# Attention's second key half rotated earlier and split later, an output-weight split moved behind the masking, and three matmuls and two splits reordered at the seam before attention

## The chip, the core and the metric

The kernel runs on one core of a Trainium2 chip. That core has a matrix engine (PE, TensorE) and four more engines that each work through their own instruction queue in order: DVE (VectorE), ACT (ScalarE), POOL (GpSimd) and SP (SyncE, which only issues transfers here). Engines wait for each other by semaphores. The metric is the device time of one execution in microseconds (us), as the median of several runs. A small letter-number such as L1318 is a line of the kernel as the profile counts it.

## The reference, cut to what matters

Two layers on 512 tokens of width 1024 in float32: a gated short convolution with its feed-forward network (FFN0), then sliding-window attention with sinks, whose keys and values are computed once from the residual stream, with its own feed-forward network (FFN1).

```python
kv = rmsnorm(h, kv_norm) @ w_kv
k_sh, v_sh = jnp.split(kv, 2, axis=-1)
k_sh = partial_rotary(k_sh.reshape(bsz, s, N_KV_HEADS, HEAD_DIM), cos, sin)
q = (rmsnorm(h, b_pre_norm[j]) @ b_w_q[j]).reshape(bsz, s, N_HEADS, HEAD_DIM)
q = partial_rotary(q, cos, sin)
attn = sliding_window_sink_attention(q, k_sh, v_sh, b_sinks[j]) @ b_w_o[j]
h = h + rmsnorm(attn, b_post_norm[j])
```

There are 16 query heads of 64 columns on 4 key heads, blocks of 128 queries, and each query block sees its own and the previous block of keys. `sliding_window_sink_attention` adds the mask to the scaled scores, takes a softmax that has one more column for the sink, and weighs the values with it.

## The kernel before, in words

**Every product is three matmuls.** A float32 operand is split into a high part (rounded by a copy on ACT) and a low part (the rest, by a subtraction on DVE or POOL). A product is then low times high, high times high and high times low, which stand as three PE rows L192, L193, L194. "Splitting" below always means this pair: first the high part on ACT, then the low part elsewhere, which waits for it.

**The seam between FFN0 and attention.** `close` runs FFN0's last product tile by tile (four tiles t of 128 tokens, two halves each, four k-steps of three matmuls in the last half that is of interest). Behind it `last_tile` finishes the residual of tile 3: `norm(t)` writes the normalised rows `xn` on ACT (L326). PE transposes these (L337, into banks `xt`) in two lots: tiles 0 and 1 inside `close`, tiles 2 and 3 later, between the matmuls of the key and value projections (`pk`, `pv`). Each transposed bank is split twice, once with the gains of the keys and values (n = 0) and once with those of the queries (n = 1), by `split(n, f, half)`: the high part on ACT at L350, the low part on DVE at L351, for one eighth f of the width. Bank b of four holds the eighths f = b and f = b + 4.

**Attention's loop.** After the seam a loop runs over steps i = 0 to 9. Each step issues the operations of the string `ORDER` in its order, each for the head pair that its offset gives: `Q` project queries, `R` rotate them, `H` split the rotated ones, `S` scores, `M` mask and take the maximum, `E` exponents, `N` normalise, `T` transpose the probabilities, `P` and `L` their high and low parts, `W` weigh the values, `O` split the result. The number behind a letter is a half or a block. There is no planner behind it. The string is the order in which every engine gets its instructions, since the scheduling is set to manual there, and each engine's queue keeps that order.

- `rope` (rotation) is a shuffle of the projection (L1244) and a product with the cosines (L1246) on DVE, then a product with the sines (L1247) and a sum (L1248) on POOL. `rope_split` is a high part on ACT (L1253) and a low part on POOL (L1254).
- `K` rotates and splits the second half of the keys once, at i = 2. The head pairs 4 to 7 read it, from i = 4 on.
- `g0` and `g1` split part of the output weights early. At i = 4 these are whole tiles (L187 on ACT, L188 on DVE), at i = 6 they are halves in slots (L181, L182). `G` splits the query weights of a later pair with the same lines L187 and L188.
- The transient tiles (`sh`, `ra`, `rhi`, `rlo`, `plo` and others) come from one pool of 35 slots, which are handed out in turn. Whoever takes a slot waits until its last reader is done.

**Names the prediction uses.** M0 and M1 are the L1318 rows that read the score banks `psc` (each with a small row that reads out the maximum). S0 and S1 write those banks (L1306). N0 and N1 are L1346, L1348 and four L1351. T0 to T3 are the L1363 transposes into `pt`. L0 to L3 are the L1380 rows. W0 to W3 are the `po` matmuls.

Of the kernel before, what the change touches and what calls it, by code (L numbers as in the profile page):

```python
# [44 lines left out]

EARLY_IN, REST_IN = 2, 0
ORDER = (
    "R- S0 T0 g0 T1 O- Q0 M0 Q1 Z0 P0 P1 S1 T2 T3 L0 Q2 L1 G M1 E00 E01 H- Q3 P2 P3 E10 E11 Z1 z0 K W0 L2 L3 A A A N0 W1 W2 N1 W3 g1 z1"
)
STEP = {  # L50
    "S": "scores", "M": "maxima", "E": "exponents", "N": "normalise", "T": "turn", "P": "high",
# [22 lines left out]
def yoco_kernel(  # L74
# [22 lines left out]
    nc = tc.nc  # L97
# [458 lines left out]
    for l in range(2):  # L556
# [3 lines left out]
        for rd, (f0, f1) in enumerate(ROUNDS[:-1]):  # L560
            k = slice(f0 // 2, f1 // 2)
# [107 lines left out]
    with tc.manual_schedule(engines=ALL):  # L669
# [25 lines left out]
        for k in range(KT):  # L695
# [7 lines left out]
            for i in range(3):  # L703
                for t in range(3):
                    n = 3 * k + t
# [9 lines left out]
        ws = [split_weights(None, raw, True) for raw in later[:2]]  # L715
# [150 lines left out]
        if square:  # L866
            res.square(t)

    def close(ws, x, k0, res, ahead, then=None, each=2):


        n = len(x) - k0

        def part(ps, t, half, ks):
            unit(ps, t, ws[len(ws) // 2 * half :], x, ks, n, k0)

        begun = [bank("pmix", ps_mm) for _ in range(2)]
        for half in range(2):
            part(begun[half], 0, half, range(n - 1))
            for _ in range(each if half == 0 or each > 1 else 0):  # L880
                ahead.one()
        for t in range(NB):
            for half in range(2):
                if t == 0:
                    ps = begun[half]
                    part(ps, t, half, range(n - 1, n))
                else:
                    ps = bank("pmix", ps_mm)
                    if (t, half) == (NB - 1, 1):
                        part(ps, t, half, range(2))  # L890
                        for b in range(4):
                            res.turn(b, (0, 1))
                        part(ps, t, half, range(2, n))
                        for f in range(4):
                            res.split(0, f, 0)
                        res.square_mix(t, 0)
                        res.square(NB - 2)
                        res.scale(t, 0)
                    else:
                        part(ps, t, half, range(n))  # L900
                res.take(t, half, ps)
                if (t, half) != (NB - 1, 0):
                    res.square_mix(t, half)
            if t < NB - 1:
                tile_done(res, t, square=t < NB - 2)
            if t == 0 and then:
                then()

    def last_tile(res, pieces, ahead=None):


        def some(i):
            for n, *f in pieces[i]:
                if n == "keep":
                    res.keep(f[0], 0, f[1])
                elif n == "weights":
                    ahead.slots()
                else:
                    res.split(n, f[0], 0)

        res.mean2(2)
        res.norm(2)
        res.mean(3)
        res.scale(3, 1)
        some(0)
        res.update(3)
        some(1)
        res.square(3)
        some(2)
        res.mean2(3)  # L930
        some(3)
        res.norm(3)
        some(4)
# [30 lines left out]
    def ffn(l, before, ahead, gain, gpres, following):  # L964
# [220 lines left out]
        if gpres:  # L1185
            ahead = Ahead(following)
            with tc.manual_schedule(engines=ALL):
                close(ws, acts[-1], 0, res, ahead)
            return res, ahead
        with tc.manual_schedule(engines=ALL):  # L1190
            for t in range(NB):
# [59 lines left out]
    def rope_split(a, eng, large=False):  # L1251
        hi, lo = halves("rhl", F32R) if large else (slot("rhi", F32R), slot("rlo", F32R))
        nc.scalar.activation(hi, a, AF.Copy)  # L1253
        eng.tensor_tensor(out=lo, in0=a, in1=hi.bitcast(F32), op=ALU.subtract)  # L1254
        return hi, lo
# [170 lines left out]
    at = []  # L1426

    with tc.manual_schedule(engines=ALL):
        last_tile(res, [[(0, 4)], [(0, 5)], [], [(0, 6), (0, 7), (1, 0), (1, 1)],
                        [(1, f) for f in (4, 5, 2, 3, 6, 7)]])  # L1430
        for hf in range(2):
            c = slice(hf * 256, (hf + 1) * 256)
            for k in range(KT):
                kk = slice(k * P, (k + 1) * P)
                for ps, (whi, wlo) in zip(pk, wk):
                    mm3(ps[:, c], whi[:, kk], wlo[:, kk], xkv[k][0][:, c], xkv[k][1][:, c],
                        k == 0, k == KT - 1)
                values(2 * hf, k)
                values(2 * hf + 1, k)
                if hf == 0 and k >= 6:  # L1440
                    for b in (2 * k - 12, 2 * k - 11):
                        res.turn(b, (2, 3))
                        res.split(0, b, 1)
            if hf == 0:
                for f in range(4, KT):
                    res.split(0, f, 1)
            if hf == 0:
                ahead.one()
                for f in range(KT):
                    res.split(1, f, 1)  # L1450
                ahead.one()
                qs[0].w, qs[1].w = ahead.ready[4:]


        vt = [halves("vt", F32R) for _ in range(NB)]
        for pair in vt:
            for v in pair:
                nc.gpsimd.memset(v.bitcast(F32), 0.0)

        last_p = [slot("lp", F32R) for i in range(2)]  # L1460
        for p in last_p:
            nc.gpsimd.memset(p.bitcast(F32), 0.0)
        for part in range(4):
            qs[0].project(part)
        ks = [rope_split(rope(pk[0], nc.vector), nc.vector)]
        qs[LEAD].weights()
        nc.scalar.activation(warm, ones[:, 0:1], AF.Exp)
        for part in range(4):
            qs[1].project(part)
        qs[0].rotate(nc.vector)  # L1470
        qs[0].split(nc.vector)
        dst = [[v.rearrange("p (h d) -> p h d", d=2 * HD)[:, :, :HD] for v in pair]
               for pair in vt]
        src = [p.rearrange("p (h d) -> p h d", d=HD) for p in pv]
        for j in range(NB):
            nc.scalar.activation(dst[j][0], src[j], AF.Copy)
        for j in range(NB):
            nc.vector.tensor_tensor(out=dst[j][1], in0=src[j], in1=dst[j][0].bitcast(F32),
                                    op=ALU.subtract)

    with tc.manual_schedule(engines=ALL):
        sum_on("a0")
        for i in range(KT + 2):
            if i == KT:
                res = Update(mix_o, B_ATT, [G_FPRE[1]])
                res.leaves = True
                ahead = Ahead(first_weights(1))
            if i == KT + 1:
                res.load()
            for c in ORDER.split():  # L1490
                if c == "A":
                    if i == KT:
                        ahead.one()
                    continue
                if c == "K":
                    if i == 2:
                        ks.append(rope_split(rope(pk[1], nc.gpsimd), nc.gpsimd))
                    continue
                late = c.endswith("-")
                op, n = c[0], [int(d) for d in c[1:].rstrip("-")]  # L1500
                t = i - late
                if op == "g":

                    u = 2 * (t - EARLY - 1) + n[0]
                    if u in (-2, -1, 2, 3):
                        j = u + 2 if u < 0 else u
                        early_w.append(split_weights(w_o[j // 2, j % 2], slots=j >= EARLY_IN))
                    continue
                if op in "SMENTPLWO":
                    t -= op in "TPLWO"  # L1510
                    of = hp
                elif op in "QRH":
                    t += LEAD
                    of = qs
                elif op == "G":
                    t += LEAD + 1
                    of = qs
                    if KT <= t < KT + 4:
                        j = t - KT
                        rest_w.append(split_weights(w_o[j // 2, 2 + j % 2], slots=j >= REST_IN))  # L1520
                else:
                    t = 2 * (t - EARLY - 1) + n.pop(0)
                    of = early
                if 0 <= t < len(of) and not (op in "RH" and t < LEAD - 1):
                    getattr(of[t], STEP[op])(*n)
                if op in "RH" and i <= KT:
                    issue(len(issues) // 2 if op == "R" else len(issues))
            if i <= KT:
                sum_on(f"a{i + 1}")
        close(rest_w, at, EARLY, res, ahead, lambda: sum_on(f"a{KT + 2}"), 1)  # L1530
# [96 lines left out]
```

## Time and profile before

| what | value |
|---|---|
| median of 3 runs | 1023.06 us (1022.95 to 1023.82) |
| the profiled execution's own time | 1023.55 us |
| its span in the profile | 1021.8 us |
| granted TensorE clock, mean | 0.998 |
| busy: PE / DVE / ACT / POOL | 1011.7 / 869.4 / 582.3 / 197.3 us |

The profiled execution is 0.49 us longer than the median of the runs, and 1.75 us of its time lie outside the span. A row of a timeline gives the start in us from the span's start, the duration in us, engine, line, operation, what it writes and reads, its shape, how many alike follow each other ("x4"), and in brackets the idle time of its engine just before it with what ended that. PE rows overlap: matmuls are pipelined, so the distance between two starts is what a matmul costs, and a wait is a distance that is longer than it is for the same work elsewhere.

### The profile page before, as it was taken

Reading aid. Unit: us, or ns where it says so; the run is one execution under the profiler, and the core shown is the slowest. Engines: PE = TensorE matmul, PEld = TensorE weight load, DVE = VectorE, ACT = ScalarE, POOL = GpSimd, SP = SyncE. Lnnn points to the kernel's source line nnn. Section 1 sums busy time; section 2 is a strip of 40 time slices with the busy share of each in tenths; the row PEclk is TensorE's granted clock in tenths of the full one; section 3 lists DMA queues with packets and bytes.
Section 4 is the critical chain, followed back from the end, with each engine's and each line's share of the span. In section 5 each row is a group of like instructions: output and inputs, shape, how many; then the busy total and the mean of one; then the engine's idle time right before and its main releaser. Section 6 shows DMA issues by size and latency. Waiting matters only on the chain.

```text
span 1021.8 us, 16273 instructions
## 1 busy us (share of the span) xinstructions
PE 1011.7 (99%) x6008; PEld 893.5 (87%) x6008; DVE 869.4 (85%) x1480; ACT 582.3 (57%) x1035; POOL 197.3 (19%) x259
## 2 busy tenths in 40 slices
PE   9999999999999999999999999999999999999997
PEld 8888888999889898998898788889998998989986
DVE  5766767899789999998869998778997899999896
ACT  6322444875655455566476676668666564645641
POOL 0443033112111111000123663231111010110001
PEclk9999999999999999999999999999999999999999
DMA  9897789549979699779404889976899676979742
GB/s 357 284 263 227 179 253 341 161 165 283 344 242 298 208 300 339 221 217 337 167 6 160 187 220 299 249 249 160 261 296 328 176 238 226 296 271 268 257 155 83
DMA packets 66575, 244.50 MB, mean 239 GB/s; under 512 B 7872, under 2 KB 8384, under 8 KB 54720
## 3 DMA queue, kind: packets, MB, share of 16 engines
q1 hardware_dynamic: 51328, 145.98, 38.7%
q0 software_dynamic: 14592, 96.48, 37.2%
q10 hardware_dynamic: 576, 1.02, 0.3%
q8 instruction: 47, 0.77, 0.3%
q14 instruction: 32, 0.26, 0.1%
HBM read 237.15 MB, written 102.76 MB: 333 GB/s over the span
## 4 chain that ended last, share of the span: by engine, by line
PE 90%; DVE 5%; ACT 2%; issue 1%; POOL 0%; DVEq 0%; ACTq 0%
PE gx L1055 14%; PE gx L1058 7%; PE pcub L193 4%; PE pcub L194 4%; PE pcub L192 4%; PE gz L194 4%; PE gz L192 4%; PE gz L193 4%; PE px L192 3%; PE px L193 3%; PE px L194 3%; PE pmix L193 2%; PE pmix L192 2%; PE pmix L194 2%; PE gy L193 2%; PE gy L192 2%
## 5 line engine op out<-in xcount | busy, mean ns | idle before, releaser
L478 DVE TENSOR_TENSOR wlo<-raw,whi 128x1024 fp32r<-128x1024 f32 x225 | 274.7, 1225 | 54.5 <-ACT whi L477 54.4
L477 ACT ACTIVATE whi<-raw 128x1024 fp32r<-128x1024 f32 x225 | 233.7, 1051 | 103.5 <-DVE raw L465 29.2
L1055 PE MATMUL gx<-xt,whi 128*128 128x512 f32 x480 | 120.4, 393 | 0.0
L1055 PEld LDWEIGHTS gx<-xt,whi 128*128 128x128 f32 x480 | 86.3, 189 | 15.5
L546 POOL DMA_DIRECT2D hsum<-in_w_gb_dram x96 | 62.9, 735 | 150.2 <-ACT whi L477 89.9
L546 POOL DMA_DIRECT2D hsum<-hsum x32 | 25.4, 792 | 291.0 <-ACT whi L477 219.4
L1017 DVE TENSOR_TENSOR st<-gx,st 128x256 f32<-128x256 f32 x200 | 77.9, 419 | 2.6 <-ACT st L1033 0.5
L1033 ACT ACTIVATE st<-gx 128x256 f32<-128x256 f32 x120 | 43.2, 380 | 62.3 <-PE gx L1058 58.7
L1058 PEld LDWEIGHTS gx<-xt,wlo 128*128 128x128 f32 x480 | 65.5, 190 | 4.7
L1058 PE MATMUL gx<-xt,wlo 128*128 128x256 f32 x480 | 66.9, 282 | 0.0
L1069 ACT ACTIVATE gr<-gr 128x1024 f32<-128x1024 f32 x20 | 21.2, 1062 | 50.2 <-DVE gr L1017 50.2
L192 PE MATMUL px<-wlo,ahi 128*128 128x512 f32 x120 | 46.8, 390 | 0.1
L194 PE MATMUL px<-whi,alo 128*128 128x512 f32 x120 | 46.7, 389 | 0.0
L193 PE MATMUL px<-whi,ahi 128*128 128x512 f32 x120 | 46.7, 389 | 0.0
L194 PE MATMUL gz<-xhi,wlo 128*128 128x256 f32 x160 | 45.5, 284 | 0.0
L192 PE MATMUL gy<-xlo,whi 128*128 128x256 f32 x160 | 45.3, 283 | 0.0
L193 PE MATMUL gy<-xhi,whi 128*128 128x256 f32 x160 | 45.3, 283 | 0.0
L192 PE MATMUL gz<-xt,whi 128*128 128x256 f32 x160 | 45.3, 283 | 0.0
L193 PE MATMUL gz<-xt,whi 128*128 128x256 f32 x160 | 45.3, 283 | 0.0
L194 PE MATMUL gy<-xhi,wlo 128*128 128x256 f32 x160 | 45.3, 283 | 0.0
L192 PE MATMUL gz<-xlo,whi 128*128 128x256 f32 x160 | 45.3, 283 | 0.0
L194 PE MATMUL gz<-xt,wlo 128*128 128x256 f32 x160 | 45.3, 283 | 0.0
(298 smaller groups left out, 2999.4 us busy)
## 6 DMA issues: line engine op xcount, KB each, us to landing
hsum<-in_w_gb_dram POOLq DMA_DIRECT2D x96, 512.0 KB, 7.8
raw<-hsum SPq DMA_DIRECT2D x88, 512.0 KB, 7.8
raw<-in_w_gb_dram SPq DMA_DIRECT2D x60, 512.0 KB, 6.7
hsum<-in_w_dn_dram POOLq DMA_DIRECT2D x36, 512.0 KB, 8.1
raw<-in_w_dn_dram SPq DMA_DIRECT2D x32, 512.0 KB, 6.5
hsum<-hsum POOLq DMA_DIRECT2D x28, 512.0 KB, 5.4
raw<-in_w_in_dram SPq DMA_DIRECT2D x21, 512.0 KB, 7.6
hsum<-in_w_dn_dram POOLq DMA_DIRECT2D x12, 768.0 KB, 12.5
```

Source lines behind the costliest of these rows:

```text
L192: nc.tensor.matmul(out, whi, xlo, start=start, stop=False, **kw)
L193: nc.tensor.matmul(out, whi, xhi, start=False, stop=False, **kw)
L194: nc.tensor.matmul(out, wlo, xhi, start=False, stop=stop, **kw)
L477: self.begun = nc.scalar.activation(hi[:, :n], raw, AF.Copy)
L478: nc.vector.tensor_tensor(out=lo[:, :n], in0=raw, in1=hi[:, :n].bitcast(F32), op=ALU.subtract)
L546: nc.gpsimd.dma_start(dst, src, max_dma_last_dim=4 * 4 * S, **kw))
L1017: nc.vector.tensor_tensor(out=out, in0=a, in1=b, op=ALU.add)
L1033: nc.scalar.activation(ste, a, AF.Copy)
L1055: nc.tensor.matmul(banks[c][e], whi[:, kk], factors[p][k][2], start=opened and k == 0, stop=False, **kw)
L1058: nc.tensor.matmul(banks[c][e][:, :256], wlo[:, kk], factors[p][k][0], start=False, stop=k == 3 and p == 4, **kw)
L1069: nc.scalar.activation(kept[2], kept[2], AF.Silu)
```

## The change

```diff
 ORDER = (
-    "R- S0 T0 g0 T1 O- Q0 M0 Q1 Z0 P0 P1 S1 T2 T3 L0 Q2 L1 G M1 E00 E01 H- Q3 P2 P3 E10 E11 Z1 z0 K W0 L2 L3 A A A N0 W1 W2 N1 W3 g1 z1"
+    "R- S0 T0 T1 O- Q0 M0 Q1 Z0 P0 P1 S1 T2 T3 L0 Q2 L1 G K M1 E00 E01 H- k g0 Q3 P2 P3 E10 E11 Z1 z0 W0 L2 L3 A A A N0 W1 W2 N1 W3 g1 z1"
 )
...
-    def close(ws, x, k0, res, ahead, then=None, each=2):
+    def close(ws, x, k0, res, ahead, then=None, each=2, lead=2):
...
                     if (t, half) == (NB - 1, 1):
-                        part(ps, t, half, range(2))
+                        part(ps, t, half, range(lead))
                         for b in range(4):
                             res.turn(b, (0, 1))
-                        part(ps, t, half, range(2, n))
+                        part(ps, t, half, range(lead, n))
...
-                close(ws, acts[-1], 0, res, ahead)
+                close(ws, acts[-1], 0, res, ahead, lead=3)
...
-        last_tile(res, [[(0, 4)], [(0, 5)], [], [(0, 6), (0, 7), (1, 0), (1, 1)],
-                        [(1, f) for f in (4, 5, 2, 3, 6, 7)]])
+        last_tile(res, [[(0, 4)], [(0, 5)], [],
+                        [(0, 6), (0, 7), (1, 0), (1, 1), (1, 4), (1, 5)],
+                        [(1, f) for f in (2, 3, 6, 7)]])
...
                 if c == "K":
                     if i == 2:
-                        ks.append(rope_split(rope(pk[1], nc.gpsimd), nc.gpsimd))
+                        rot_k = rope(pk[1], nc.gpsimd)
+                    continue
+                if c == "k":
+                    if i == 3:
+                        ks.append(rope_split(rot_k, nc.gpsimd))
                     continue
```

Nothing is computed differently, and no instruction is added or removed. There are four moves. `K` now only rotates, ahead of `M1` at i = 2, and the new `k` splits, behind `H-` at i = 3. `g0` moves from ahead of `O-` and `M0` to behind `k`, which matters at i = 4 and at i = 6. At the seam the sixteen transposes of tiles 0 and 1 stand behind three instead of two of the four k-steps. And the query splits of eighths 4 and 5 stand ahead of `norm(3)` instead of behind it.

PE's queue at the seam, before (`pmix` is FFN0's last product, `xt_5168` and its successors are the transposed banks):

```order
L192 MATMUL pmix_5161<-wlo_4850,ahi_4613 128x512
L193 MATMUL pmix_5161<-whi_4848,ahi_4613 128x512
L194 MATMUL pmix_5161<-whi_4848,alo_4614 128x512
L337 MATMUL xt_5168<-ident,xn_5103 128x128
L337 MATMUL xt_5168<-ident,xn_5143 128x128
```

The same place in the changed kernel:

```order
L194 MATMUL pmix_5161<-whi_4848,alo_4614 128x512
L192 MATMUL pmix_5161<-wlo_4897,ahi_4839 128x512
L193 MATMUL pmix_5161<-whi_4895,ahi_4839 128x512
L194 MATMUL pmix_5161<-whi_4895,alo_4840 128x512
L337 MATMUL xt_5171<-ident,xn_5103 128x128
L337 MATMUL xt_5171<-ident,xn_5143 128x128
```

One k-step of three matmuls now lies ahead of the first transpose. `xn_5103` and `xn_5143` are the normalised tiles 0 and 1.

ACT's queue a little later at the seam, as a piece of the difference (`xn_5257` before and `xn_5265` after is the normalised tile 3, `xt_5168` or `xt_5171` is bank 0, `xt_5173` or `xt_5176` bank 1):

```order
-L326 ACTIVATE xn_5257<-h_5000,ur_4990 128x1024
-L350 ACTIVATE xhi_5259<-xt_5168,gt 128x256
-L350 ACTIVATE xhi_5263<-xt_5173,gt 128x256
+L350 ACTIVATE xhi_5257<-xt_5171,gt 128x256
+L350 ACTIVATE xhi_5261<-xt_5176,gt 128x256
+L326 ACTIVATE xn_5265<-h_5000,ur_4990 128x1024
```

The normalising of tile 3 went behind two of the query splits. DVE's own order is the same there.

DVE's queue at step i = 2, before, from the low part of `G` on (`pk` is the key projection's second half, `plo_6007` the low part of L2):

```order
L188 TENSOR_TENSOR wlo_6022<-raw_6019,whi_6021 128x1024
L1318 ISA s_6026,nm_6025<-psc_5987,mask,nsnk 128x256
L1318 ISA nm_6025 128x1
L1318 ISA s_6027,nm_6025<-psc_5988,mask,nsnk 128x256
L1318 ISA nm_6025 128x1
L1318 ISA s_6026,nm_6025<-psc_5987,mask,nsnk 128x256
L1318 ISA nm_6025 128x1
L1318 ISA s_6027,nm_6025<-psc_5988,mask,nsnk 128x256
L1318 ISA nm_6025 128x1
L1244 STREAM_SHUFFLE sh_6061<-pk_5213 128x512
L1246 TENSOR_TENSOR ra_6063<-pk_5213,ctab_5216 128x512
L1380 TENSOR_TENSOR plo_6007<-pt_6001,phi_6006 128x512
```

The same stretch in the changed kernel:

```order
L188 TENSOR_TENSOR wlo_6022<-raw_6019,whi_6021 128x1024
L1244 STREAM_SHUFFLE sh_6025<-pk_5213 128x512
L1246 TENSOR_TENSOR ra_6027<-pk_5213,ctab_5216 128x512
L1318 ISA s_6032,nm_6031<-psc_5987,mask,nsnk 128x256
L1318 ISA nm_6031 128x1
L1318 ISA s_6033,nm_6031<-psc_5988,mask,nsnk 128x256
L1318 ISA nm_6031 128x1
L1318 ISA s_6032,nm_6031<-psc_5987,mask,nsnk 128x256
L1318 ISA nm_6031 128x1
L1318 ISA s_6033,nm_6031<-psc_5988,mask,nsnk 128x256
L1318 ISA nm_6031 128x1
L1380 TENSOR_TENSOR plo_6007<-pt_6001,phi_6006 128x512
```

The two DVE rows of the key rotation went ahead of M1. In the order with its waits, `plo_6007` waited before for ACT's high part and for the last of the first six `po` matmuls on PE (W0), which was the last reader of the slot that it got. In the changed kernel it gets another slot, and it waits for ACT's high part and for a POOL row of the query rotation before.

POOL's queue at i = 2 and i = 3, before (`hsum` rows are transfers of FFN1's weights that POOL issues, `rhl` is a query's low part):

```order
L546 DMA hsum_178<-hsum_176 64x2048
L1254 TENSOR_TENSOR rhl_6040<-ra_5929,rhl_6040 128x512
L546 DMA hsum_180<-in_w_gb_dram 64x2048
L546 DMA hsum_181<-in_w_gb_dram 64x2048
L1247 TENSOR_TENSOR sh_6061<-sh_6061,stab_5217 128x512
L1248 TENSOR_TENSOR ra_6063<-ra_6063,sh_6061 128x512
L1254 TENSOR_TENSOR rlo_6068<-ra_6063,rhi_6067 128x512
L1247 TENSOR_TENSOR sh_6112<-sh_6112,stab_5217 128x512
```

And now:

```order
L546 DMA hsum_178<-hsum_176 64x2048
L1247 TENSOR_TENSOR sh_6025<-sh_6025,stab_5217 128x512
L1248 TENSOR_TENSOR ra_6027<-ra_6027,sh_6025 128x512
L1254 TENSOR_TENSOR rhl_6046<-ra_5929,rhl_6046 128x512
L546 DMA hsum_180<-in_w_gb_dram 64x2048
L546 DMA hsum_181<-in_w_gb_dram 64x2048
L1247 TENSOR_TENSOR sh_6108<-sh_6108,stab_5217 128x512
L1248 TENSOR_TENSOR ra_6110<-ra_6110,sh_6108 128x512
L546 DMA hsum_179<-hsum_178 64x2048
L1254 TENSOR_TENSOR rhl_6221<-ra_6110,rhl_6221 128x512
L546 DMA hsum_182<-in_w_gb_dram 64x2048
L546 DMA hsum_183<-in_w_gb_dram 64x2048
```

The key rotation's two POOL rows stand ahead of the query's low part and of two transfers, and the key's own low part `rlo` follows only after the last row shown, one step later.

`g0` moves in the same way on ACT (L187) and DVE (L188) at i = 4: on DVE its row goes from between L1246 and L1401 (ahead of M0) to between M1's last row and L2's L1380, and on ACT from ahead of L1400 to behind the rotated query's high part L1253. At i = 6 the same holds for the L181 and L182 rows. On SP the load of one query-weight tile now goes out ahead of the first output-weight tile.

## The prediction

> **What bounds the kernel now.** I read the page first, its busy times.
>
> ```profile
> PE 1011.7 (99%) x6008; PEld 893.5 (87%) x6008; DVE 869.4 (85%) x1480; ACT 582.3 (57%) x1035; POOL 197.3 (19%) x259
> ```
>
> PE is the bound, and the change leaves its work alone. So only places count where PE waits for another engine. I went through PE's timeline in the two stretches that the change touches, looking for starts that lie further apart than the same work elsewhere. This is the attention loop, i = 2 to 4:
>
> ```profile
> 573.39 0.39 PE L194 MATMUL pq<-xhi,wlo 128*128 128x512 f32 x1
> 574.61 0.87 PE L1363 MATMUL pt<-ident,s 128*128 128x128 f32 x6
> ...
> 579.37 0.28 PE L194 MATMUL po<-phi,vt 128*128 128x256 f32 x1
> 579.77 0.39 PE L192 MATMUL po<-plo,vt 128*128 128x256 f32 x1
> ...
> 582.30 0.55 PE L1363 MATMUL pt<-ident,s 128*128 128x128 f32 x3
> ...
> 583.93 0.59 PE L1363 MATMUL pt<-ident,s 128*128 128x128 f32 x3 [0.23 <-DVE s L1351]
> 584.28 0.48 PE L192 MATMUL pq<-xlo,whi 128*128 128x512 f32 x1
> ...
> 586.91 0.39 PE L194 MATMUL pq<-xhi,wlo 128*128 128x512 f32 x1
> 587.59 0.76 PE L1306 MATMUL psc<-rlo,rhl 64*128 64x256 f32 x2 [0.29 <-DVE nm L1318]
> 588.86 0.87 PE L1363 MATMUL pt<-ident,s 128*128 128x128 f32 x6
> ...
> 593.76 0.28 PE L192 MATMUL po<-plo,vt 128*128 128x256 f32 x1
> ...
> 596.20 1.09 PE L1363 MATMUL pt<-ident,s 128*128 128x128 f32 x8
> 597.04 0.48 PE L192 MATMUL pq<-xlo,whi 128*128 128x512 f32 x1
> 599.65 0.39 PE L194 MATMUL pq<-xhi,wlo 128*128 128x512 f32 x1
> 601.60 0.87 PE L1363 MATMUL pt<-ident,s 128*128 128x128 f32 x6
> ```
>
> There are four waits. (a) Ahead of W2 at i = 2: 0.40 between 579.37 and 579.77, where a `po` matmul costs 0.12 (its neighbours' distance), and the first one runs 0.39 instead of 0.28, so 0.28 + 0.10 = 0.38. (b) T0 and T1, eight transposes: 582.30 to 584.28 is 1.98, against 596.20 to 597.04, 0.84, so 1.14. (c) S1 at i = 3: last projection to first transposition 586.91 to 588.86, 1.95, against 573.39 to 574.61, 1.22, so 0.73. (d) S1 at i = 4: 599.65 to 601.60, 1.95 again, 0.73. Together 2.98 us. The other engines tell why:
>
> ```profile
> 573.57 1.21 DVE L188 TENSOR_TENSOR wlo<-raw,whi 128x1024 fp32r<-128x1024 f32 x1
> ...
> 576.45 0.74 DVE L1244 STREAM_SHUFFLE sh<-pk 128x512 f32<-128x512 f32 x1
> ...
> 579.02 0.69 DVE L1380 TENSOR_TENSOR plo<-pt,phi 128x512 fp32r<-128x512 f32 x1 [1.26 <-ACT se L1341]
> ...
> 579.96 0.97 DVE L1346 TENSOR_TENSOR se<-se,rs 128x4 f32<-128x4 f32 x1
> 581.18 2.03 DVE L1351 TENSOR_SCALAR s<-s,rd 128x128 f32<-128x128 f32 x4
> 583.13 0.15 DVE L1346 TENSOR_TENSOR se<-se,rs 128x4 f32<-128x4 f32 x1
> ...
> 586.42 0.34 DVE L1318 CUSTOM_DVE_ANT_0 s<-psc,mask,nsnk 128x128 f32<-128x128 f32 x1
> ...
> 593.05 1.01 DVE L1351 TENSOR_SCALAR s<-s,rd 128x128 f32<-128x128 f32 x4
> 596.67 1.97 DVE L188 TENSOR_TENSOR wlo<-raw,whi 128x1024 fp32r<-128x1024 f32 x1
> ...
> 599.16 0.34 DVE L1318 CUSTOM_DVE_ANT_0 s<-psc,mask,nsnk 128x128 f32<-128x128 f32 x1
> ...
> 604.46 0.68 DVE L1380 TENSOR_TENSOR plo<-pt,phi 128x512 fp32r<-128x512 f32 x1
> ```
>
> ```profile
> 577.69 1.86 POOL L1247 TENSOR_TENSOR sh<-sh,stab 128x512 f32<-128x512 f32 x1
> 579.63 1.28 POOL L1248 TENSOR_TENSOR ra<-ra,sh 128x512 f32<-128x512 f32 x1
> 581.66 1.40 POOL L1254 TENSOR_TENSOR rlo<-ra,rhi 128x512 fp32r<-128x512 f32 x1 [0.74 <-ACT rhi L1253]
> ```
>
> (a): DVE stands 1.26 ahead of L2's row at 579.02. The row names ACT, but the built order names W0's sixth matmul as well, for the slot, and the time fits that. (b): DVE begins N0 at 579.96, and L1346 on four columns takes 0.97 instead of 0.15 (583.13). It ends when POOL's sum does (579.63 + 1.28 = 580.91). The four L1351 take 2.03 instead of 1.01 while POOL's key split runs. So N0 is late by 0.8 + 1.0 through POOL, behind the 1.26. (c): M0 starts at 586.42 and frees the score banks too late; it inherits (b). (d): `g0`'s L188 stands ahead of M0 and takes 1.97 instead of 1.21.
>
> The seam:
>
> ```profile
> 509.24 0.27 PE L337 MATMUL xt<-ident,xn 128*128 128x128 f32 x1
> 509.73 1.86 PE L337 MATMUL xt<-ident,xn 128*128 128x128 f32 x15 [0.22 <-ACT xn L326]
> ...
> 522.75 0.28 PE L194 MATMUL pv<-whi,xlo 128*128 128x256 f32 x1
> 523.28 1.06 PE L337 MATMUL xt<-ident,xn 128*128 128x128 f32 x8 [0.24 <-DVE xlo L351]
> ```
>
> ```profile
> 511.72 0.47 DVE L351 SCALAR_TENSOR_TENSOR xhl<-xt,gt,xhl 128x256 fp32r<-128x256 f32 x1
> ...
> 520.15 1.66 DVE L351 SCALAR_TENSOR_TENSOR xlo<-xt,gt,xhi 128x256 fp32r<-128x256 f32 x4 [0.21 <-ACT xhi L350]
> ```
>
> ```profile
> 520.37 0.84 ACT L350 ACTIVATE xhi<-xt,gt 128x256 fp32r<-128x256 f32 x2
> 521.09 1.17 ACT L326 ACTIVATE xn<-h,ur 128x1024 f32<-128x1024 f32 x1
> 522.13 1.58 ACT L350 ACTIVATE xhi<-xt,gt 128x256 fp32r<-128x256 f32 x4
> 523.95 0.87 ACT L350 ACTIVATE xhi<-xt,gt 128x256 fp32r<-128x256 f32 x2 [0.24 <-DVE xlo L351]
> ```
>
> PE waits twice: 0.49 ahead of the second transpose (pitch 0.84 / 8 = 0.105) for tile 1's `xn`, 0.38 lost; and 522.75 to 523.28, 0.53 instead of 0.12, 0.41 lost, for the low part of query eighth 4, which frees the bank.
>
> **The change part by part.**
>
> *Third k-step ahead of the first transposes.* Its three matmuls, about 0.68, cover wait one: gain 0.38. The splits of tiles 0 and 1 then start some 0.2 later on ACT. DVE's first low part starts only at 511.72, though its bank was transposed by 510.4 (509.73, three more at 0.105, and a duration of 0.27) and its high part takes 0.4 to 0.5. So DVE has some 0.8 to spare, and I let nothing pass on; bounds 0 and +0.2.
>
> *Query splits ahead of tile 3's `xn`.* ACT and DVE read one bank in turn: the pair at 523.95 waited for DVE. So eighth 4's high part waits for the low part of eighth 0, the third of the four rows from 520.15, which ends near 521.40, and eighth 5's for 521.81. They run 521.45 to 521.9 and 521.86 to 522.33, and `xn` 522.25 to 523.42 instead of 521.09 to 522.26. Bank 0 is free by 522.5, but the second transpose needs tile 3 and starts near 523.45. Before, it started some 0.1 behind 523.28. So PE leaves this place 0.05 later than before, whatever it saved at 509: the seam nets +0.05. Bounds: −0.4 if the splits need not wait that way, +0.4 if `xn` is late by one more split (1.58 / 4).
>
> *Rotation ahead of M1 at i = 2.* On DVE two rows go ahead, 1.2 to 1.3 together (from 576.45 until the wait of 1.26 ahead of 579.02 begins, 577.76); M1 ends 1.2 later, and L2 comes at about 577.6 without the slot's wait, ending 578.25. W2 is due at 579.49: (a) goes. On POOL the products run at 575.5 to 578.1 beside M1, which reads a score bank (rows that read such a bank are not held: L2's row at 579.02 took 0.69 beside POOL's product and sum). The query's low part moves to 578.2 to 579.5, and S0 needs it near 580.9 (its eight rows take 1.22 − 0.23 = 0.99 ahead of 582.30, and PE runs 0.38 earlier). It holds N0's first row until 579.6. N0's L1351 end at 580.85 and N1's, a little longer, at 582.3. T0 is due at 582.30 − 0.38 = 581.92, its N0 rows done: (b) goes. Two transfers of FFN1's weights leave POOL some 3 us later; FFN1 comes after six more steps, so I take nothing, with +0.4 (the size of (a)) as the bound.
>
> *Key split at i = 3.* M0 follows N1 by three rows (shuffle, product and L1401, of one size, so 1.83 with 0.61 each), so it starts at 584.13 and frees its first bank as before 587.59 − 586.42 = 1.17 later, 585.3. S1 is due at 581.92 + (599.65 + 0.23 − 596.20) = 585.6. So (c) goes, with 0.3 to spare. The split's POOL row, 1.3 long, comes about where N0 of that step begins, and I let it hold N0 by 1.1. N0's four rows began at 593.05 before, so 593.05 − 2.25 + 1.1 = 591.9 now; they end at 592.9, and N1's, a 0.35 for its small rows later, at 594.4, the first two near 593.8. T0 is due at 596.20 − 2.25 = 593.95, and its sixth transpose, the first to read N1, at 594.5: nothing, bound +0.3.
>
> *g0 behind k, at i = 4.* Without L188 M0 follows N1 by 1.83: 596.2, banks free 597.4. S1 is due at 599.88 − 2.25 = 597.63: (d) goes, with 0.2 to spare. The moved L188 (1.13 from start to start) now stands between M0 and L2, which were 604.46 − 599.16 = 5.30 apart. So L2 starts at 596.2 + 5.30 + 1.13 = 602.6 and ends at 603.3. W2 stood 593.76 − 587.59 = 6.17 behind a held S1 at i = 3, which is near 5.9 behind one that isn't (0.73 − 0.45 of the wait lay behind its start), due at 597.63 + 5.9 = 603.5: nothing, with 0.2 to spare. The ACT row, at most 1.2 long like its partner, goes ahead of L2's high part, which can start at 599.5 (601.60 − 2.98 + 0.87) and is then done by 601.4, ahead of 602.6. At i = 6 the two L182 rows move likewise; no PE wait stands there before, so nothing, bounds ±0.2. SP's exchanged loads: no wait quoted here is for a load, so nothing, bound +0.4 as above.
>
> The sum: −2.98 + 0.05, and 0.1 for leftovers where PE restarts, −2.8 us. Against the profiled execution: 1023.55 − 2.8 = 1020.75. The median lies 0.49 below that execution, so 1020.3.
>
> *A rule weighed.* The row of 0.97 ending with POOL's sum is the measured side. The Trainium skill, "SBUF — State Buffer", section "SBUF: two separate sides", says that VectorE (with two SBUF inputs) and GpSimd share a port pair as an exclusive lock, and that whichever starts first holds it for the whole instruction. The trace agrees in the 0.97. By that rule alone a POOL row that starts just ahead of the moved L188 would hold it for a whole POOL row; the trace of before has no such meeting at i = 4. What that would cost is the second rival.
>
> **The rivals.** *The margins don't hold.* M0 at i = 3 and 4 has 0.3 and 0.2 to spare, and this rests on some eight rows in a chain. If both waits stay by half or more, 0.7 to 1.4 of the gain is lost: about 1021.5. For it: both margins are a quarter of one POOL row; against: each row was taken as long as its like in the same trace.
>
> *The moved g0 meets POOL.* At i = 4 the query's low part runs on POOL after three transfers, and L188 is due at 601.5. Held from 0.3 up to a whole 1.28, L2 ends at 603.6 to 604.6, and W2 waits 0.1 to 1.0: 1020.4 to 1021.3, and T0 later perhaps as much again.
>
> *Slots, slower.* Two slots of the pool of 35 are now taken earlier and one is held a step longer, so every later taker gets another slot. If L2's 1.26 wait appears at other steps, each occurrence costs (a) + (b) + (c) = 2.25. The gain is gone at 1.3 occurrences, and from three on it is slower: 1020.3 + 6.75 = 1027.0. Against it: in the built order the waits of these rows name only rows long done.
>
> *The seam gains too.* If ACT need not wait for DVE at 521.4, the first saving stays: 1019.8.
>
> **How the numbers follow.** A change of 0.2% is 2.05 us, about what can be told from none here, so faster means below 1021.0. My forecast of 1020.3 has 0.50, the seam's gain 0.06, the margins 0.20 (0.16 of it above 1021.0), the collision 0.09 (0.03 of it above 1021.0), slots or another new wait 0.15 (0.10 of it above 1025.1, the rest between). Faster 0.50 + 0.06 + 0.04 + 0.06 = 0.66, same 0.16 + 0.03 + 0.05 = 0.24, slower 0.10. The range: from 1019.5, where the seam gains and a little more, to 1022.3, where the margins fail and the collision comes on top; left out are the slots and what lies beyond.
>
> **What would show it.** In the changed profile the second transpose near 509 follows the first by 0.1, and the one near 523 still waits, now for ACT's `xn`. DVE stands no 1.26 ahead of L2 at i = 2. N0's L1351 there take about 1.0, and no PE row at `pt` or `psc` at i = 3 and 4 names DVE. The prediction is wrong if a row of the loop that waited for nothing now names DVE or POOL, above all W2 at i = 4, or if the steps i = 5 to 9 get longer.

## The result, and the profile after

The changed kernel takes 1020.32 us (median of 8 runs, 1019.89 to 1020.72), the kernel before 1023.18 us (median of 8 runs, 1022.87 to 1023.82). The ratio is 0.9971, with a 95% interval of 0.9961 to 0.998: 0.29% faster. The profiled execution took 1020.30 us at a span of 1018.5 us and a clock of 0.998. One execution of a version below, "turns by tile", took 3554.58 us in a slow state and is left out of the median given for it.

The page of the changed kernel, its busy times:

```profile
PE 1009.5 (99%) x6008; PEld 892.5 (88%) x6008; DVE 867.7 (85%) x1480; ACT 581.5 (57%) x1035; POOL 195.0 (19%) x259
```

PE's timeline of the changed kernel at the places of the four waits (a) to (d), in order:

```profile
579.11 0.28 PE L194 MATMUL po<-phi,vt 128*128 128x256 f32 x1
579.23 0.28 PE L192 MATMUL po<-plo,vt 128*128 128x256 f32 x1
...
581.67 1.09 PE L1363 MATMUL pt<-ident,s 128*128 128x128 f32 x8
582.52 0.48 PE L192 MATMUL pq<-xlo,whi 128*128 128x512 f32 x1
...
585.13 0.39 PE L194 MATMUL pq<-xhi,wlo 128*128 128x512 f32 x1
585.44 0.39 PE L1306 MATMUL psc<-rlo,rhl 64*128 64x256 f32 x2
...
586.35 0.87 PE L1363 MATMUL pt<-ident,s 128*128 128x128 f32 x6
...
597.12 0.39 PE L194 MATMUL pq<-xhi,wlo 128*128 128x512 f32 x1
...
598.34 0.87 PE L1363 MATMUL pt<-ident,s 128*128 128x128 f32 x6
```

The matmul ahead of W2 is followed after 0.12 (before: 0.40). The eight transposes stand in one group and take 0.85 until the next projection (before: 1.98). Both S1 stretches take 1.22 (before: 1.95). No row there names DVE any more.

DVE and POOL in the changed kernel, the rows that answer to those of before:

```profile
577.28 0.68 DVE L1380 TENSOR_TENSOR plo<-pt,phi 128x512 fp32r<-128x512 f32 x1
577.88 0.41 DVE L1380 TENSOR_TENSOR lp<-pt,lp 128x256 fp32r<-128x256 f32 x1
578.21 0.99 DVE L1346 TENSOR_TENSOR se<-se,rs 128x4 f32<-128x4 f32 x1
...
579.45 1.01 DVE L1351 TENSOR_SCALAR s<-s,rd 128x128 f32<-128x128 f32 x4
...
583.66 0.34 DVE L1318 CUSTOM_DVE_ANT_0 s<-psc,mask,nsnk 128x128 f32<-128x128 f32 x1
...
589.89 1.04 DVE L1346 TENSOR_TENSOR se<-se,rs 128x4 f32<-128x4 f32 x1
...
595.39 0.35 DVE L1318 CUSTOM_DVE_ANT_0 s<-psc,mask,nsnk 128x128 f32<-128x128 f32 x1
...
600.69 1.23 DVE L188 TENSOR_TENSOR wlo<-raw,whi 128x1024 fp32r<-128x1024 f32 x1
601.83 0.69 DVE L1380 TENSOR_TENSOR plo<-pt,phi 128x512 fp32r<-128x512 f32 x1
```

```profile
577.89 1.29 POOL L1254 TENSOR_TENSOR rhl<-ra,rhl 128x512 fp32r<-128x512 f32 x1
...
589.60 1.31 POOL L1254 TENSOR_TENSOR rlo<-ra,rhi 128x512 fp32r<-128x512 f32 x1
...
599.12 1.38 POOL L1254 TENSOR_TENSOR rhl<-ra,rhl 128x512 fp32r<-128x512 f32 x1
```

L2's low part no longer has an idle time ahead of it. N0's first row is still held twice, once by the query's low part (0.99, ending at 579.20 with POOL's 577.89 + 1.29 = 579.18) and once, at i = 3, by the moved key split (1.04, ending at 590.93 with 589.60 + 1.31 = 590.91). Neither reaches PE. The moved L188 starts at 600.69, when POOL's row of that step has ended (599.12 + 1.38 = 600.50), and takes its plain 1.23.

The seam in the changed kernel, PE and then ACT:

```profile
509.66 1.91 PE L337 MATMUL xt<-ident,xn 128*128 128x128 f32 x16
...
522.05 0.28 PE L194 MATMUL pv<-whi,xlo 128*128 128x256 f32 x1
522.31 0.30 PE L337 MATMUL xt<-ident,xn 128*128 128x128 f32 x1
523.13 0.98 PE L337 MATMUL xt<-ident,xn 128*128 128x128 f32 x7 [0.52 <-ACT xn L326]
```

```profile
521.17 0.87 ACT L350 ACTIVATE xhi<-xt,gt 128x256 fp32r<-128x256 f32 x2 [0.24 <-DVE xlo L351]
521.94 1.14 ACT L326 ACTIVATE xn<-h,ur 128x1024 f32<-128x1024 f32 x1
```

The first wait is gone (sixteen transposes in one group), and the second is longer: the second transpose follows 0.82 behind the first and names ACT's `xn`. ACT stood 0.24 ahead of the two query splits for DVE, as forecast, and the normalising came behind them.

**Where the time went, by place.** Executions differ by up to 0.9 us in their first 47 us, where the same instructions run in all kernels, so two spans compare poorly at this scale. I took the start of the same PE matmul, by its place in PE's queue, from each profiled execution, and subtracted that of before. The marks are a matmul of FFN0's last product (493.82 before), one behind the seam (531.03), a transpose of T1 at i = 3 (583.93), a projection behind S1 at i = 3 (590.50), a transpose behind S1 at i = 4 (602.10), and the last matmul. The table gives what each stretch between two marks took beyond the kernel before, in us (minus is faster). "Start" is the difference at the first mark, and "sum" is what follows up to the start of the last matmul. Each row comes from one execution.

| kernel | start | seam | to T1, i = 3: (a), (b) | S1, i = 3: (c) | S1, i = 4: (d) | rest | sum |
|---|---|---|---|---|---|---|---|
| the change | −0.26 | +0.03 | −1.43 | −0.86 | −0.74 | +0.02 | −2.98 |
| order alone | −0.68 | +0.01 | −1.44 | −0.86 | −0.74 | 0.00 | −3.03 |
| seam alone | −0.12 | +0.05 | −0.01 | 0.00 | −0.01 | −0.02 | +0.01 |
| lead alone | −0.56 | −0.02 | −0.01 | +0.01 | −0.02 | −0.04 | −0.07 |
| keys alone | +0.13 | 0.00 | −1.43 | −0.86 | +0.68 | +0.01 | −1.61 |
| g0 alone | +0.02 | 0.00 | −0.02 | 0.00 | −0.73 | −0.02 | −0.77 |
| split only | −0.47 | −0.01 | −1.41 | −0.08 | +0.88 | −0.02 | −0.63 |
| split undone | −0.78 | +0.04 | +0.35 | +0.01 | −0.73 | −0.04 | −0.37 |
| turns by tile | −0.40 | +0.01 | −1.44 | −0.86 | −0.74 | −0.04 | −3.07 |
| turns and order | −0.75 | −0.36 | −1.43 | −0.86 | −0.74 | 0.00 | −3.40 |

The mark at T1 lies some transposes ahead of the end of that wait, so a little of (b) falls into the next column; (a), (b) and (c) together are −2.29, where the sum had 2.25. A zero here means that the whole stretch repeats to within a few hundredths, so differences of 0.1 can be read from it, which the times alone don't allow.

The table does not see what lies behind the last matmul. From its start to the end of the span it took 7.05 to 7.11 us in nine of the eleven profiled executions, but 7.45 in g0 alone and 7.25 in split only. Of the profiled execution's time, 2.1 us lie outside the span in keys alone and 1.9 in split only, against 1.75 before. These 0.2 to 0.4 us are not at a place that the edits touch, and why they differ stays open. They are one reason why the times of these three versions fall short of their rows in the table.

### The profile page after: what moved, and what is told of

It reads as the page before. It is cut to its first block, busy times and chain, and to the rows that moved or that the text cites. A ratio compares the mean times of both kernels' runs of the same rounds, so it can differ in the third digit from the quotient of the medians.

```text
span 1018.5 us, 16274 instructions
## 1 busy us (share of the span) xinstructions
PE 1009.5 (99%) x6008; PEld 892.5 (88%) x6008; DVE 867.7 (85%) x1480; ACT 581.5 (57%) x1035; POOL 195.0 (19%) x259
## 3 DMA queue, kind: packets, MB, share of 16 engines
q10 hardware_dynamic: 576, 1.02, 0.3%
## 4 chain that ended last, share of the span: by engine, by line
PE 93%; DVE 3%; ACT 2%; issue 1%; DMA 0%; POOL 0%; DVEq 0%; SPq 0%; ACTq 0%
PE gx L1055 14%; PE gx L1058 7%; PE pcub L192 4%; PE pcub L194 4%; PE pcub L193 4%; PE gz L194 4%; PE gz L192 4%; PE gz L193 4%; PE px L192 3%; PE px L193 3%; PE px L194 3%; PE pmix L193 2%; PE pmix L192 2%; PE pmix L194 2%; PE gy L194 2%; PE gy L192 2%
```

## The experiments

**Which part makes the gain: the order alone and the seam alone.** "Order alone" has the new string and the new branch `k` and leaves `close` and `last_tile` as they were. "Seam alone" is the reverse.

```diff
 order alone
-    "R- S0 T0 g0 T1 O- ... G M1 E00 E01 H- Q3 ... z0 K W0 ..."
+    "R- S0 T0 T1 O- ... G K M1 E00 E01 H- k g0 Q3 ... z0 W0 ..."
...
 seam alone
-                close(ws, acts[-1], 0, res, ahead)
+                close(ws, acts[-1], 0, res, ahead, lead=3)
...
+                        [(0, 6), (0, 7), (1, 0), (1, 1), (1, 4), (1, 5)],
+                        [(1, f) for f in (2, 3, 6, 7)]])
```

> Only the order string with K, k and g0 is changed, the seam is as before. Theory (all of the gain comes from the four waits in the attention loop): 2.9 to 3.1 us less than before, the same time as the full change within 0.15 us, and PE still waits 0.4 near 509 and 0.4 near 523. Rival (the seam's reordering contributes): less than 2.6 us gained, 0.4 us slower than the full change.

> Only the third k-step ahead of the transposes and the two query splits ahead of the normalising, attention's order as before. Theory: the 0.4 us saved near 509 comes back near 522, so 0 to +0.1 us against before. Rival (the first saving stays): 0.35 to 0.45 us less.

Order alone: 1020.05 us against 1023.23, ratio 0.997 (0.9959 to 0.9982). Seam alone: 1023.56 us against 1023.23, ratio 1.0006 (0.9998 to 1.0015). All of the gain comes from attention's order, and the seam's two edits together are worth nothing, as the table says (+0.03 and +0.05). By the medians order alone gains 3.18, a little over the 3.1 that I expected, and ends 0.27 below the change instead of within 0.15; the table has it within 0.05. PE still waits at both places of the seam there. The median of seam alone is 0.33 above the kernel before, which its interval doesn't tell from nothing. PE's timeline of seam alone shows the exchange, the first wait gone and the second one for ACT:

```profile
509.80 1.91 PE L337 MATMUL xt<-ident,xn 128*128 128x128 f32 x16
...
522.48 0.30 PE L337 MATMUL xt<-ident,xn 128*128 128x128 f32 x1
523.29 0.98 PE L337 MATMUL xt<-ident,xn 128*128 128x128 f32 x7 [0.52 <-ACT xn L326]
```

**The third k-step alone.** Only `lead=3`, with the query splits behind the normalising as before.

> Only the third k-step ahead of the first transposes. Theory: the wait near 509 goes, PE comes 0.4 us earlier to the second lot of transposes and waits 0.4 us longer there for the low part of query eighth 4, which ends when it did: 0 against before within 0.1. Rival: 0.35 to 0.45 us less.

1023.01 us against 1023.08, ratio 0.9999 (0.999 to 1.0008), and −0.02 at the seam in the table. PE's timeline of it:

```profile
509.36 1.91 PE L337 MATMUL xt<-ident,xn 128*128 128x128 f32 x16
...
521.75 0.28 PE L194 MATMUL pv<-whi,xlo 128*128 128x256 f32 x1
522.71 1.06 PE L337 MATMUL xt<-ident,xn 128*128 128x128 f32 x8 [0.67 <-DVE xlo L351]
```

PE comes earlier by the saved 0.4 and waits 0.96 instead of 0.53 at the same place, for the same DVE row. The bound there is the residual's chain on DVE and ACT, which the transposes' place doesn't move. With this edit the second edit only changes whom PE waits for; no run has the second edit by itself.

**The two edits of the order apart.** "Keys alone" moves `K` and `k` and leaves `g0`; "g0 alone" moves only `g0`.

> Only the key rotation moved ahead of M1 and its split moved to i = 3; g0 and the seam as before. Theory: waits (a), (b) and (c) go, 2.25 us less than before; the wait (d) of 0.73 us at S1 of i = 4 stays, with g0's L188 ahead of M0. Rival (the three waits are not one chain): S1 at i = 3 still waits, 1.5 us less.

> Only g0 moved behind H, the keys and the seam as before. Theory: only wait (d) goes, 0.73 us less than before, and (a), (b), (c) stand as they did. Rival (the moved L188 meets POOL's query split and delays W2): 0 to 0.5 us less, and PE waits ahead of W2 at i = 4.

Keys alone: 1022.01 us against 1023.23, ratio 0.9988 (0.9979 to 0.9997). g0 alone: 1023.03 us against 1023.23, ratio 0.9997 (0.9989 to 1.0006). Both fell short of what I expected in the times. In the table g0 alone gains what was expected (−0.77), and 0.37 of it is given back behind the last matmul. Keys alone gains 1.61 instead of 2.25, and this is a real miss. The rival's 1.5 lies near it, but not for the rival's reason: S1 at i = 3 no longer waits (−0.86). (a), (b) and (c) go, but wait (d) does not stay at 0.73: it grows. PE, DVE and POOL of keys alone at i = 4:

```profile
598.84 0.76 PE L1306 MATMUL psc<-rlo,rhl 64*128 64x256 f32 x2 [0.98 <-DVE nm L1318]
```

```profile
589.97 1.31 POOL L1254 TENSOR_TENSOR rlo<-ra,rhi 128x512 fp32r<-128x512 f32 x1
...
596.15 2.14 POOL L1248 TENSOR_TENSOR ra<-ra,sh 128x512 f32<-128x512 f32 x1
```

```profile
590.25 1.07 DVE L1346 TENSOR_TENSOR se<-se,rs 128x4 f32<-128x4 f32 x1
...
595.18 1.98 DVE L188 TENSOR_TENSOR wlo<-raw,whi 128x1024 fp32r<-128x1024 f32 x1
...
597.67 0.34 DVE L1318 CUSTOM_DVE_ANT_0 s<-psc,mask,nsnk 128x128 f32<-128x128 f32 x1
```

DVE has no idle time in this trace from 573.65 to M0 at 597.67, so it is the bound of that stretch. M0 came 1.49 earlier than in the kernel before (599.16) while PE came 2.16 earlier, and the difference of 0.67 is what wait (d) grew by. What DVE lost is the moved key split: from M0 at i = 3 (584.02, before 586.42) to M0 at i = 4 it took 13.65 instead of 12.74, 0.91 more, and N0's first row at 590.25 took 1.07 instead of 0.15 beside POOL's split. So the two parts are worth −1.61 and −0.77 alone, and −3.03 together: 0.65 more than their sum. On top of the moved keys the move of `g0` gains 1.42, alone 0.77.

The rival of g0 alone, that the moved L188 meets POOL's query split, came true without a cost. DVE and POOL of g0 alone at i = 4:

```profile
602.61 1.48 DVE L188 TENSOR_TENSOR wlo<-raw,whi 128x1024 fp32r<-128x1024 f32 x1
```

```profile
601.70 1.30 POOL L1254 TENSOR_TENSOR rhl<-ra,rhl 128x512 fp32r<-128x512 f32 x1 [0.67 <-ACT rhl L1253]
```

L188 takes 1.48 instead of 1.22, since POOL's row runs until 603.00. L2's low part comes that much later, and PE does not wait for it: the stretch gains its −0.73 and the rest of the kernel stays as it was (−0.02).

**Which half of the key's move: only the split later, and only the rotation earlier.** "Split only" leaves the rotation behind M1 and the transfers and moves the split to i = 3. "Split undone" is the full change with the split back at i = 2, ahead of W0.

```diff
 split only (against before)
-    "... E00 E01 H- Q3 ..."
+    "... E00 E01 H- k Q3 ..."
...
 split undone (against the change)
-    "... H- k g0 Q3 ... z0 W0 ..."
+    "... H- g0 Q3 ... z0 k W0 ..."
...
-                    if i == 3:
+                    if i == 2:
```

> Only the key split moved to i = 3; the rotation, g0 and the seam as before. L2's low part at i = 2 then gets a slot that is long free. Theory (slot wait and POOL's hold are two separate causes): DVE stands no 1.26 us ahead of L2 and wait (a) goes, but the rotation's two POOL rows still hold N0 until about 580.9, so a part of (b) and (c) stays, 0.9 to 1.8 us less than before. Rival 1 (only the slot counts): 2.25 us less. Rival 2 (only POOL's place counts): 0 to 0.4 us less.

> The full change, but the key split stays at i = 2 ahead of W0, where the two slots it takes leave L2's low part with the slot that W0 frees. Theory: DVE's wait ahead of L2 comes back, (a) returns with 0.38, and the split's POOL row holds N0, so a part of (b) and (c) returns, 1.0 to 2.0 us slower than the full change. Rival (the early rotation alone makes the gain): the same as the full change within 0.2 us.

Split only: 1023.1 us against 1023.08, ratio 0.9999 (0.999 to 1.0008). Split undone: 1022.77 us against 1023.08, ratio 0.9997 (0.9989 to 1.0006), and 2.45 us slower than the full change. In the table split only gains 1.41 up to T1 and gives 0.88 back at S1 of i = 4; split undone loses all of (a) to (c) and a little more. Split only missed its expectation of 0.9 to 1.8: the medians differ by nothing, as its second rival had it, and the table has 0.63. Up to S1 at i = 3 it gains 1.49, inside that range, so the second rival's reason does not hold. What I had left out is that wait (d) then grows by 0.88, as in keys alone, because `g0` stands ahead of M0 here too. The rows of split only at i = 2, DVE and POOL:

```profile
577.19 0.68 DVE L1380 TENSOR_TENSOR plo<-pt,phi 128x512 fp32r<-128x512 f32 x1
...
579.34 1.89 DVE L1351 TENSOR_SCALAR s<-s,rd 128x128 f32<-128x128 f32 x4
```

```profile
579.14 1.29 POOL L1248 TENSOR_TENSOR ra<-ra,sh 128x512 f32<-128x512 f32 x1
```

L2's low part has no idle time ahead of it, though the rotation stands where it did. So the wait of 1.26 came from the slots that the key split took. In the built programs the key split's high part takes the slot that L2's low part gets in split only and in the changed kernel. With the split at i = 2, in the kernel before and in split undone, L2's low part gets a slot two turns on, whose last readers are W0's matmuls. The POOL hold is the other cause, seen alone here: the four L1351 take 1.89 beside POOL's sum instead of 1.01. That hold no longer reached T0 and T1, but it reached M0, and S1 at i = 3 kept its wait (−0.08). At i = 4 L188 and M0 stand so, DVE and then PE:

```profile
595.57 1.98 DVE L188 TENSOR_TENSOR wlo<-raw,whi 128x1024 fp32r<-128x1024 f32 x1
...
598.07 0.34 DVE L1318 CUSTOM_DVE_ANT_0 s<-psc,mask,nsnk 128x128 f32<-128x128 f32 x1
```

```profile
599.24 0.76 PE L1306 MATMUL psc<-rlo,rhl 64*128 64x256 f32 x2 [1.17 <-DVE nm L1318]
```

Split undone, with the rotation early, has both back:

```profile
578.26 0.69 DVE L1380 TENSOR_TENSOR plo<-pt,phi 128x512 fp32r<-128x512 f32 x1 [1.41 <-ACT se L1341]
...
579.20 2.36 DVE L1346 TENSOR_TENSOR se<-se,rs 128x4 f32<-128x4 f32 x1
```

```profile
579.67 1.85 POOL L1254 TENSOR_TENSOR rlo<-ra,rhi 128x512 fp32r<-128x512 f32 x1
```

PE's sixth matmul of W0 in split undone:

```profile
577.88 0.28 PE L194 MATMUL po<-phi,vt 128*128 128x256 f32 x1
```

The wait is back for the slot: in the built order L2's row names W0's matmul again, which ends at 577.88 + 0.28 = 578.16, just ahead of L2's 578.26. And N0's first row, four columns wide, takes 2.36, until POOL's split ends at 581.52. I had expected 1.0 to 2.0 us, and it was 2.45 by the medians and 2.6 by the table. That the hold would be longer than one POOL row was not in my working.

**Can the seam give something after all?** In "turns by tile" PE transposes tile 2 of two banks ahead of tile 3, so that part of the work fits into the wait for tile 3. "Turns and order" moves also the key split of eighth 7 behind the two query splits of eighths 0 and 1, so that ACT and DVE don't meet at one bank.

```diff
 turns by tile (against the change)
-                    for b in (2 * k - 12, 2 * k - 11):
-                        res.turn(b, (2, 3))
-                        res.split(0, b, 1)
+                    for ts in ((2,), (3,)):
+                        for b in (2 * k - 12, 2 * k - 11):
+                            res.turn(b, ts)
+                    for b in (2 * k - 12, 2 * k - 11):
+                        res.split(0, b, 1)
...
 turns and order, in addition
-                        [(0, 6), (0, 7), (1, 0), (1, 1), (1, 4), (1, 5)],
+                        [(0, 6), (1, 0), (1, 1), (0, 7), (1, 4), (1, 5)],
```

> The full change, and in the second lot of transposes PE does tile 2 of both banks ahead of tile 3. Theory: PE's wait near 522 is for tile 3's normalised rows alone (ACT), with tile 2 and both banks ready by 522.6, so three more transposes of 0.11 us fit into the wait: 0.3 us less than the full change. Rival (the banks come free late as well): the same as the full change within 0.1 us.

> The full change with PE's transposes of tile 2 ahead of those of tile 3, as in the run before, and with the key split of eighth 7 behind the query splits of eighths 0 and 1, so that ACT needs not wait 0.24 us for DVE there. In the run before the 0.3 us gained at the first two banks was lost again at the other two, which DVE's low parts of eighths 2, 3, 6 and 7 free too late. Theory (ACT's and DVE's chain sets the second lot of transposes): the whole chain comes 0.2 to 0.25 us earlier, and PE leaves the seam 0.2 to 0.4 us earlier than with the full change, both measured from the same PE row ahead of the seam. Rival (the chain is set by tile 3's normalising, not by ACT's queue): 0 to 0.1 us.

Turns by tile: 1020.20 us (six executions) against 1023.08, ratio 0.9971 (0.996 to 0.9982), the same as the change. Turns and order: 1020.09 us against 1023.28, ratio 0.9968 (0.9956 to 0.998). PE, ACT and DVE of turns by tile:

```profile
522.18 1.47 PE L337 MATMUL xt<-ident,xn 128*128 128x128 f32 x8
525.00 1.24 PE L337 MATMUL xt<-ident,xn 128*128 128x128 f32 x8
```

```profile
523.87 0.87 ACT L350 ACTIVATE xhi<-xt,gt 128x256 fp32r<-128x256 f32 x2 [0.19 <-DVE xlo L351]
```

```profile
524.37 0.88 DVE L351 SCALAR_TENSOR_TENSOR xlo<-xt,gt,xhi 128x256 fp32r<-128x256 f32 x2
```

The 0.3 was there at the first two banks and was lost at the other two: their transposes now come at 525.00, and the low parts that free those banks run until 524.37 + 0.88 = 525.25. In turns and order ACT runs its six splits without a break and the normalising starts earlier:

```profile
518.91 2.28 ACT L350 ACTIVATE xhi<-xt,gt 128x256 fp32r<-128x256 f32 x6
521.08 1.16 ACT L326 ACTIVATE xn<-h,ur 128x1024 f32<-128x1024 f32 x1
```

The seam then takes 0.36 less than before, 0.39 less than in the change, near the upper end of what was expected. So ACT's and DVE's chain sets the seam, and that version is the fastest of all by the trace (−3.40). Its median is 0.23 us under that of the change, which the times can't tell from nothing. No run has the new order of the splits without the transposes by tile, so what the order is worth by itself stays open.

## Why the prediction was right

The forecast was 1020.3 us, and 1020.32 was measured. The waits it named went, for the reasons it gave, but that the two figures meet to 0.02 is luck. The median of the same kernel before was 1023.06 in one set of runs and 1023.18 in the other, and the gain of 2.8 was 2.86 by the medians and 2.98 in the trace.

- *(a), (b), (c), the keys.* Forecast −2.25, measured −2.29. DVE's wait ahead of L2 went, N0's four rows took 1.01, and M0 came in time. The reason given for (a), the slot, was named from the built order against the profile's own label (ACT); split only and split undone confirm it. N0's first row is still held at i = 2 (0.99), now by the query's low part, as the prediction had it.
- *(d), g0.* Forecast −0.73, measured −0.74. What the prediction left unsaid is that this wait is not a fixed size. With the keys' move alone it grew to 1.4, since the moved key split holds N0 at i = 3, so the two parts needed each other. The sum came out right because it was worked for both together: M0's start was taken from N1's end in the changed order, not from the old wait.
- *The seam.* Forecast +0.05, measured +0.03, by the steps given: 0.38 gained at the first transposes, ACT's 0.24 for DVE at the shared bank, `xn` behind the two splits, the second transpose waiting for it.
- *The margins* that the first rival stood on were larger than I worked out. The first score bank was free at 584.68 with S1 at 585.44, 0.76 instead of 0.3, and at 596.42 with S1 at 597.44, 1.0 instead of 0.2. The forecast took 1.17 from M0's start to the bank's release, which was the distance to PE's next start; the release itself came after 1.02. N0's hold at i = 3 also ended some 0.5 earlier than assumed.
- *The meeting of g0 with POOL* did not come, by 0.19 (600.50 against 600.69). That rival was near: in g0 alone the meeting came and held L188 by 0.26.
- *The allowance of 0.1* for leftovers was not needed: −2.98 in the trace, where the terms without it add up to −2.93.
- *The slot rival*, a new slot wait elsewhere, did not appear: the rest of the kernel is within 0.02.

## What to carry to other kernels

A wait that is removed early in a stretch is only gained if the engine waited for also comes earlier at the next meeting; work the later waits out in the new order instead of subtracting them one by one, since here two edits were worth 1.6 and 0.8 alone and 3.0 together. A long record of a tiny row on DVE was a wait in disguise here, and the cure was to move POOL's rows beside work of DVE that wasn't held (M1, which reads score banks). Where a saving comes back as a wait a few microseconds later, as at the seam, the bound is a chain on other engines, and only an edit that shortens that chain helps.

## What the runs showed of the hardware

- Rows of DVE that read and write SBUF alone (L1346, L1351, L188) were held while POOL computed, and the hold shows as the row's own duration, not as idle time: an addition of four columns took 0.15 alone, 0.97 to 1.07 against one POOL row, and 2.36 in split undone; four L1351 took 1.89 to 2.03 instead of 1.01, and L188 1.97 instead of 1.21. Rows that read PSUM beside POOL took their usual time (L1380: 0.68). The hold goes the other way too: in the kernel before, POOL's L1248 at 597.63 took 2.15 instead of 1.28, beside DVE's L188 of 1.97. The 2.36 began 0.47 ahead of the recorded start of POOL's row. That row's 1.85 includes 0.54 in which the record of a transfer that POOL issued still ran (until 580.21); where the two records don't overlap, as at 589.60 in the changed kernel, the row took 1.31. The issue of a transfer by itself did not hold the addition elsewhere: in the changed kernel it took 0.15 at 580.37 beside the record of one. So what held DVE ahead of POOL's row stays open. The rule of the Trainium skill, "SBUF — State Buffer", section "SBUF: two separate sides", that one side blocks the other for a whole instruction, agrees with the 0.97 to 1.07, which end with POOL's row; no run here separates it from another cause in the 2.36.
- The first 47 us of the program differ by up to 0.9 us between executions with the same instructions, while stretches behind them repeat to a few hundredths. Comparing by place in PE's queue resolved effects that the intervals of the times (about ±0.9 us) didn't.
